# Down products by column quarters for all groups, and row tiles for the last expert's rows

## The chip, the cores and the metric

The kernel runs on one core of one Trainium2 chip. The metric is the device time of one execution in microseconds. Three runs are shown, and one further execution was profiled.

## What is computed

A trunk of two decoder layers over 256 tokens of width 1024, all in float32: retention and a dense SwiGLU, then a short convolution and a mixture of experts, then a final norm. The change lies in the mixture of experts (and in the last additions and the norm behind it):

```python
def _moe_swiglu(xn, w_router, w_gate_e, w_up_e, w_down_e):
    ...
    top_vals, top_idx = lax.top_k(logits, TOP_K)          # 2 of 8 experts for a token
    top_w = jax.nn.softmax(top_vals, axis=-1)
    gates = jnp.sum(jax.nn.one_hot(top_idx, N_EXPERTS, dtype=jnp.float32) * top_w[..., None], axis=1)
    for e in range(N_EXPERTS):
        h = jax.nn.silu(t @ w_gate_e[e]) * (t @ w_up_e[e])        # 1024 -> 3584
        out = out + gates[:, e:e + 1] * (h @ w_down_e[e])         # 3584 -> 1024
```

## The kernel before

Each expert takes up to 96 of its tokens (CAP) into fixed slots, as three groups of 32. A one-hot product (`gather`) brings the tokens into the slots, and at the end another (`scatter`, two products of 512 columns and one addition to `h` on VectorE) brings the slots' rows back to the tokens.

The experts are worked through in 56 steps s, 7 for each expert e (u = 0 to 6), each on 512 of the 3584 hidden columns. In step s TensorE first does gate and up of this step (`moe_gate_up`: 96 products, each with a stationary tile of 128 x 32 and 256 moving columns), then down of the step before (`moe_down`: 48 products). In the profile a product is two instructions. Four products, one for each of TensorE's four column tiles of 32, form a quad. In gate/up the four share their stationary tile, the 32 slots of one group, and take four column ranges of the weights. In down three column tiles belong to the three groups (columns r = 0, 1, 2 of 256), and the fourth takes column quarter 3 for group r:

```python
for r in range(3):
    o = accs[r // 2][:, r % 2 * 256:r % 2 * 256 + 256]
    for t in range(4):
        g, c = (t, r) if t < 3 else (r, 3)
```

So after seven steps the rows of all 96 slots lie in their own partitions for columns 0 to 767, and only quarter 3 lies in partitions 96 to 127, group beside group. `scale_y` (called at the end of step u = 0 of the next expert) copies these to `yraw`, moves them by three transfers of ScalarE's queue (L694) into `yq`, and scales and splits the other 768 columns straight from the accumulators into `yH` and `yL` (the rounded part, on ScalarE, and the remainder, on VectorE). What it returns, `rest`, does the same with `yq`.

Weights come in pieces of 1 MB through 14 buffers (`raw`). Each piece is loaded by SyncE's queue (L107) as soon as TensorE has read the piece that was in its buffer: `moe_piece` stands behind each quarter of gate/up and each half of down. Behind the quarters of gate/up stand the hooks 0 to 3, a table by hand (`extras`): hook 0 transposes the hidden rows of the step before (`moe_hid_T`, with a copy on ScalarE); at u = 1 hooks 1 and 2 scatter the first 512 columns of the expert before, and hook 3 is `rest`; at u = 2 hooks 1 and 2 scatter the other 512. Gathers, slots and gates of the next experts stand in other steps. Instructions run on each engine in the order of the program. The last expert ends with `scale_y`, `scatter`, `rest`, `scatter`, the squares for the norm, and the stores.

Of the kernel before, what the change touches and what calls it, by code (L numbers as in the profile page):

```python
# [53 lines left out]
class Trunk:  # L54
# [20 lines left out]
    def moe_pools(self):  # L75

        self.dense.close()
        pool = lambda name, **k: self.ctx.enter_context(self.tc.tile_pool(name=name, reuse_waits="tile", **k))
        self.xp = pool("x", bufs=1, side="right")
        self.gup = pool("gu", bufs=4, space=bass.MemoryType.PSUM)  # L80
        self.accp = pool("macc", bufs=2, space=bass.MemoryType.PSUM)
        self.psp = pool("mps", bufs=2, space=bass.MemoryType.PSUM)

# [479 lines left out]
    def moe(self, base, ev, mp):  # L563
# [61 lines left out]
        fr = small("fr", [1])  # L625

        def overflow1():
            nc.vector.tensor_scalar(fl, pos, CAP - 0.5, None, op0=OP.is_gt)
            nc.vector.tensor_tensor(fl, fl, sel, op=OP.mult)
            nc.vector.tensor_reduce(fr, fl, axis=AX.XY, op=OP.add)  # L630

        def overflow2():
            p = self.ps()
            self.mm(p[:, 0:1], ones, fr, True, True)
            self.ovf = mp.tile([P, 1], I32, name="ovf")
            return lambda: nc.vector.tensor_copy(self.ovf, p[:, 0:1])
# [47 lines left out]
        def scale_y(e, accs):  # L684


            g = GS[e // 2][0:CAP, e % 2:e % 2 + 1]
            yH, yL = (self.xp.tile([P, D], F32R, name=n) for n in ("yH", "yL"))
            raw = self.xp.tile([P, 768], F32, name="yraw")
            q = self.xp.tile([P, 256], F32, name="yq")  # L690
            nc.vector.tensor_copy(raw[CAP:P, 0:512], accs[0][CAP:P, :])
            nc.vector.tensor_copy(raw[CAP:P, 512:768], accs[1][CAP:P, 0:256])
            for i in range(NG):
                nc.scalar.dma_start(q[32 * i:32 * i + 32], raw[CAP:P, 256 * i:256 * i + 256])  # L694
            for a, n, at in ((accs[0], 512, 0), (accs[1], 256, 512)):
# [41 lines left out]
        def extras(s):  # L737

            e, u = divmod(s, MU)
            pr = e // 2  # L740
            if s == 0:
                return {1: gates1}
            if s == 1:
                return {1: gates2}
            if s == 2:
                return {1: overflow1, 2: lambda: overflow2()()}
            if e and u in (1, 2):
                hf = u - 1
                f = {1: lambda: scatter(e - 1, hf, 0), 2: lambda: scatter(e - 1, hf, 1)}
                if u == 1:  # L750
                    f[3] = late.pop(e - 1)
                elif e % 2 and pr < 3:
                    def nxt():
                        PS[pr + 1] = new_oneh()
                        one_hot(pr + 1, PS[pr + 1])
                        row_factors(pr + 1)
                    f[3] = nxt
                return f
            if u > 2 and (e == 0 or e % 2 and pr < 3):
                a = (0, (1,)) if e == 0 else (pr + 1, (0, 1))  # L760
                f = {q: (lambda kb: lambda: gather(a[0], kb, a[1]))(2 * u - 7 + q) for q in (1, 2)}
                if e == 0 and u == 3:
                    f[3] = lambda: slots(0)
                if e == 0 and u == 4:
                    f[3] = lambda: slot_gates(0)
                return f
            if e and e % 2 == 0 and u == 5:
                return {1: lambda: slots(pr), 2: lambda: slot_gates(pr)}
            return {}

        at = base
        hid = accs = None
        for s in range(MU * NE):
# [5 lines left out]
            if s == COUNT_AT:  # L779
                n_over = nc.values_load(self.ovf[0:1, 0:1], min_val=0, max_val=NE * S)  # L780
            o = self.moe_gate_up(at, XP[e // 2][:, :, e % 2], hooks)
            at += 4
            new = self.moe_swiglu(o)
            if hid is not None:
                if u == 1:
# [42 lines left out]
    def moe_piece(self, at, hook=None):  # L828

        if at not in self.extra:  # L830
            self.dma_next()
        if hook is not None:
            hook()

    def moe_gate_up(self, at, X, hooks):


        A, B = (self.gup.tile([P, 512], F32, name="gu") for _ in range(2))
        o = (A[:, 0:256], A[:, 256:512], B[:, 0:256])
        for q in range(4):  # L840
            w = self.raw[at + q].rearrange("p (k j c) -> p k j c", k=2, j=4)
            for k in range(2):
                kb = 2 * q + k
                for g in range(NG):
# [3 lines left out]
            self.moe_piece(at + q, hooks.get(q))  # L848
        return A.rearrange("p (g u c) -> p g u c", g=2, u=2), B[:, 0:256].rearrange("p (g u c) -> p g u c", g=1, u=2)

    def moe_swiglu(self, o):
        nc = self.nc
        sg, hid = (self.xp.tile([P, NG, P], F32, name=n, bufs=2) for n in ("sg", "hid"))
# [46 lines left out]
    def over(self, low, wm, mp, pos, gts, rs, tH, tL, iota):  # L900
        nc, tc = self.nc, self.tc
        with tc.For_i(0, NE, 1) as e:
# [33 lines left out]
            acc = [self.bank(), self.bank()]  # L936
# [6 lines left out]
            for u in range(MU):  # L943
                o = [self.gup.tile([P, 512], F32, name="gu") for _ in range(2)]
# [165 lines left out]
```

## Time and profile before

| | |
|---|---|
| median of three runs (lowest to highest) | 1546.11 us (1545.5 to 1546.37) |
| profiled execution, its own time | 1545.94 us |
| its span, first to last instruction | 1544.2 us |
| busy: TensorE, weight loads, VectorE, ScalarE | 98%, 67%, 28%, 22% |
| HBM read | 449.68 MB |
| mean granted clock of TensorE | 0.992 |

Times are microseconds from the start of the span. An engine's busy time is the union of its instructions. A granted clock of 1.0 is 2.4 GHz. PE is TensorE, PEld its weight loads, DVE VectorE, ACT ScalarE, POOL GpSimd, SP SyncE; a q behind a name (ACTq, SPq) is the engine's instruction queue, which issues the transfers.

### The profile page before, as it was taken

The page shows a single profiled execution, that of the slowest core. Times are in us where ns is not written, and L with a number is a line of the kernel's source. Part 1 is how long each engine was busy: PE and PEld are TensorE (multiplying, and loading weights), DVE is VectorE, ACT ScalarE, POOL GpSimd, SP SyncE. Part 2 cuts the span into 40 slices and gives each one's busy share as a digit, 9 for nine tenths or more (in the row PEclk, how much of TensorE's full clock was granted, in tenths as well). Part 3 has the DMA queues.
Part 4 walks back from the last instruction along what each step waited for, and adds up shares of the span by engine and source line. Part 5 has one row for each costly group of instructions (what it writes and reads, how often), then busy time and mean ns, then how long its engine had stood idle before and what let it go on. Part 6 is the DMA issues. An engine that isn't in the chain of part 4 may idle for free.

```text
span 1544.2 us, 41832 instructions
## 1 busy us (share of the span) xinstructions
PE 1520.5 (98%) x19502; PEld 1032.4 (67%) x19503; DVE 427.2 (28%) x702; ACT 336.6 (22%) x568; POOL 20.3 (1%) x28
## 2 busy tenths in 40 slices
PE   9999999999999999999999999999999999999995
PEld 7888888888889965555555555555555555555552
DVE  6656665545567630001001001001001101001002
ACT  5444454434454320000000001001001001000001
POOL 0000000000000020000000000000000000000000
PEclk9999999999999999999999999999999999999997
DMA  9845455454545458999999999999999999999960
GB/s 378 357 172 192 140 188 190 179 204 164 191 165 191 178 209 325 341 375 350 354 355 380 384 369 379 346 363 374 365 368 397 352 356 366 371 371 385 358 255 32
DMA packets 65844, 454.28 MB, mean 294 GB/s; under 512 B 7936, under 2 KB 9472, under 8 KB 11520
## 3 DMA queue, kind: packets, MB, share of 16 engines
q1 hardware_dynamic: 63072, 449.34, 76.8%
q8 instruction: 154, 2.52, 0.6%
q10 hardware_dynamic: 2592, 2.20, 0.5%
q14 instruction: 26, 0.21, 0.0%
HBM read 449.68 MB, written 1.05 MB: 292 GB/s over the span
## 4 chain that ended last, share of the span: by engine, by line
PE 97%; DVE 1%; issue 0%; ACT 0%; DMA 0%; POOL 0%; ACTq 0%; SPq 0%; POOLq 0%
PE gu L141 39%; PE acc L141 28%; PE ps L141 27%; PE ps L863 2%; PE ps L331 0%; DMA raw<-in_w 0%; PE ps L188 0%; PE ps L362 0%; PE ps L227 0%; ACT wh L119 0%; POOL xT L809 0%; PE ps L668 0%; ACT junk L208 0%; ACTq L694 0%; PE ps L552 0%
## 5 line engine op out<-in xcount | busy, mean ns | idle before, releaser
L141 PE MATMUL gu<-raw,X 128*32 128x256 f32 x10752 | 615.6, 380 | 0.0
L141 PEld LDWEIGHTS gu<-raw,X 128*32 128x32 f32 x10752 | 336.8, 110 | 232.6 <-issue 20.0
L141 PE MATMUL acc<-raw,hT 128*32 128x256 f32 x5280 | 295.1, 379 | 0.6 <-ACT hT L865 0.6
L141 PEld LDWEIGHTS acc<-raw,hT 128*32 128x32 f32 x5280 | 171.0, 110 | 114.0 <-ACT hT L865 0.9
L122 DVE TENSOR_TENSOR wl<-raw,wh 128x1024 fp32r<-128x1024 f32 x180 | 213.0, 1221 | 39.6 <-ACT wh L119 39.4
L119 ACT ACTIVATE wh<-raw 128x1024 fp32r<-128x1024 f32 x180 | 182.3, 1055 | 80.8 <-PE ps L141 41.7
L141 PE MATMUL ps<-wh,xT 128*128 128x512 f32 x704 | 196.0, 400 | 2.3 <-ACT wh L119 2.3
L141 PEld LDWEIGHTS ps<-wh,xT 128*128 128x128 f32 x704 | 130.7, 189 | 32.5 <-ACT wh L119 2.6
L856 DVE TENSOR_TENSOR hid<-gu,sg 128x256 f32<-128x256 f32 x112 | 34.8, 353 | 397.0 <-ACT sg L855 397.0
L855 ACT ACTIVATE sg<-gu 128x256 f32<-128x256 f32 x112 | 36.7, 330 | 402.9 <-PE gu L141 400.9
L865 ACT ACTIVATE hT<-ps 128x384 f32<-128x384 f32 x56 | 27.4, 490 | 387.6 <-PE ps L863 387.6
L141 PE MATMUL ps<-wl,xT 128*128 128x512 f32 x352 | 111.2, 397 | 0.0
L141 PE MATMUL ps<-xT,wh 128*128 128x256 f32 x640 | 88.8, 280 | 0.5 <-DVE xT L159 0.5
L141 PEld LDWEIGHTS ps<-xT,wh 128*128 128x128 f32 x640 | 81.4, 188 | 1.6 <-ACT xT L157 0.7
L141 PEld LDWEIGHTS ps<-wl,xT 128*128 128x128 f32 x352 | 66.2, 188 | 16.4 <-DVE wl L122 0.5
L651 DVE SCALAR_TENSOR_TENSOR X<-ps,gT,rrow 128x192 f32<-128x192 f32 (+1 forms) x40 | 15.1, 378 | 223.0 <-PE ps L141 222.5
L709 DVE TENSOR_TENSOR h<-h,ps 128x512 f32<-128x512 f32 x32 | 21.9, 688 | 132.2 <-PE ps L141 132.2
L141 PE MATMUL ps<-xT,wl 128*128 128x256 f32 x320 | 50.6, 280 | 0.1
L141 PE MATMUL acc<-wh,hH 128*128 128x512 f32 x112 | 44.0, 393 | 0.0
L141 PE MATMUL acc<-wh,hL 128*128 128x512 f32 x112 | 43.8, 391 | 0.0
L141 PEld LDWEIGHTS ps<-xT,wl 128*128 128x128 f32 x320 | 43.2, 188 | 0.3 <-DVE wl L122 0.3
L141 PE MATMUL acc<-wh,xT 128*128 128x512 f32 x144 | 38.9, 398 | 0.0
(155 smaller groups left out, 754.6 us busy)
## 6 DMA issues: line engine op xcount, KB each, us to landing
raw<-in_w SPq DMA_DIRECT2D x421, 1024.0 KB, 6.5
raw<-in_w SPq DMA_DIRECT2D x6, 512.0 KB, 6.5
xT<-in_w SPq DMA_DIRECT2D x2, 1024.0 KB, 6.0
h<-in_x SPq DMA_DIRECT2D x4, 256.0 KB, 5.0
out<-xT SPq DMA_DIRECT2D x4, 256.0 KB, 2.7
mask<-in_cst ACTq DMA_DIRECT2D x4, 192.0 KB, 4.4
yq<-yraw ACTq DMA_DIRECT2D x24, 32.0 KB, 6.7
xT<-in_gfin SPq DMA_DIRECT2D x1, 512.0 KB, 9.3
```

What stands on the lines that cost most here:

```text
L119: self.nc.scalar.activation(h, r, AF.Copy)
L122: eng.tensor_tensor(l, r, h.bitcast(F32), op=OP.subtract)
L141: self.nc.tensor.matmul(out, lhsT, rhs, start=start, stop=stop)
L651: nc.vector.scalar_tensor_tensor(XP[pr][:, kb, a:b], o, self.gT[:, 3, kb:kb + 1], RR[pr][:, a:b], op0=OP.mult, op1=OP.mult)
L709: nc.vector.tensor_tensor(self.h[:, tb, f], self.h[:, tb, f], p, op=OP.add)
L855: nc.scalar.activation(sg[:, f], p[:, :, 0], AF.Silu)
L856: nc.vector.tensor_tensor(hid[:, f], p[:, :, 1], sg[:, f], op=OP.mult)
L863: self.nc.tensor.transpose(p[:, g], hid[:, g], self.ident)
L865: self.nc.scalar.activation(T, p, AF.Copy)
```

## The change

- Down: column tile q takes column quarter q, for every group. The four products of a quad share their stationary tile.
- So the rows of an expert lie by column quarter in the partitions, and every one has to be moved. `scale_y` copies both accumulators whole, and ScalarE issues twelve transfers (four quarters by three groups, 32 KB each). `rest` scales and splits all 1024 columns. It is hook 2 of u = 1; the scatters are hook 3 of u = 1 and hooks 1 to 3 of u = 2.
- The last expert has no transfers: `last_slots` repeats its slots in four row tiles, and `last_scatter` brings each column quarter to the tokens from the partitions that it lies in.
- In a step the order is now gate/up of groups 0 and 1 (with the hooks), down of groups 0 and 1, down of group 2, gate/up of group 2. The calls of `moe_piece` all stand behind these.
- The gathers and the one-hot of the next pair move to hooks of u = 3 to 5. PSUM tiles become fixed ones, three products with zeros clear banks at the start, and the overflow count becomes nine flags.

```diff
-        self.gup = pool("gu", bufs=4, space=bass.MemoryType.PSUM)
-        self.accp = pool("macc", bufs=2, space=bass.MemoryType.PSUM)
+        gup = pool("gu", bufs=1, space=bass.MemoryType.PSUM)
+        self.gu = [[gup.tile([P, 512], F32, name=f"gu{i}{j}") for j in "ab"] for i in range(2)]
+        self.macc = [gup.tile([P, 512], F32, name=f"macc{i}") for i in range(2)]
         self.psp = pool("mps", bufs=2, space=bass.MemoryType.PSUM)
+        for t in (self.gu[0][1], self.gu[1][1], self.macc[1]):
+            self.nc.tensor.matmul(t, self.zero[:, 0:P], self.zero, start=True, stop=True)
...
-        def scale_y(e, accs):
-
-
-            g = GS[e // 2][0:CAP, e % 2:e % 2 + 1]
-            yH, yL = (self.xp.tile([P, D], F32R, name=n) for n in ("yH", "yL"))
-            raw = self.xp.tile([P, 768], F32, name="yraw")
-            q = self.xp.tile([P, 256], F32, name="yq")
-            nc.vector.tensor_copy(raw[CAP:P, 0:512], accs[0][CAP:P, :])
-            nc.vector.tensor_copy(raw[CAP:P, 512:768], accs[1][CAP:P, 0:256])
-            for i in range(NG):
-                nc.scalar.dma_start(q[32 * i:32 * i + 32], raw[CAP:P, 256 * i:256 * i + 256])
-            for a, n, at in ((accs[0], 512, 0), (accs[1], 256, 512)):
-                f = slice(at, at + n)
-                self.split(yH[0:CAP, f], yL[0:CAP, f], a[0:CAP, 0:n], g)
-            Y[e] = yH, yL
+        def scale_y(e):
+
+            raw = self.xp.tile([P, NG, 256], F32, name="yraw")
+            y = self.xp.tile([P, D], F32, name="y")
+            nc.vector.tensor_copy(raw[:, 0:2].rearrange("p g c -> p (g c)"), self.macc[0])
+            nc.vector.tensor_copy(raw[:, 2], self.macc[1][:, 0:256])
+            for q in range(4):
+                for g in range(NG):
+                    nc.scalar.dma_start(y[32 * g:32 * g + 32, 256 * q:256 * q + 256], raw[32 * q:32 * q + 32, g])
 
             def rest():
-                self.split(yH[0:CAP, 768:D], yL[0:CAP, 768:D], q[0:CAP], g)
+                Y[e] = [self.xp.tile([P, D], F32R, name=n) for n in ("yH", "yL")]
+                self.split(Y[e][0][0:CAP], Y[e][1][0:CAP], y[0:CAP], GS[e // 2][0:CAP, e % 2:e % 2 + 1])
             return rest
+
+        def last_slots(tb):
+
+            if tb == 0:
+                t = self.com.tile([P, 4, NG, P], F32R, name="xT", bufs=3)
+                PT[8], four = t[:, 0:2], t[:, 2:4]
+                PS[8] = four.bitcast(F32)
+                for i in range(2):
+                    o = PS[3].bitcast(F32)[:, i, 1, 0:CAP].rearrange("p (g t) -> p g t", g=NG)
+                    nc.vector.tensor_copy(four[:, i].rearrange("p g (q t) -> p g q t", q=4),
+                                          o[:, :, None, :].to_broadcast([P, NG, 4, 32]))
+            p = self.ps()
+            for g in range(NG):
+                nc.tensor.transpose(p[:, g * P:(g + 1) * P], PS[8][:, tb, g], self.ident)
+            nc.scalar.activation(PT[8][:, tb], p[:, 0:NG * P].rearrange("p (g t) -> p g t", g=NG), AF.Copy)
+
+        def last_gates():
+            p = self.ps()
+            for g in range(NG):
+                for tb in range(2):
+                    self.mm(p[:, g:g + 1], PS[8][:, tb, g], gts[:, tb, 7:8], tb == 0, tb == 1)
+            GS[8] = mp.tile([P, NG], F32, name="gs4")
+            nc.vector.tensor_copy(GS[8], p[:, 0:NG])
+
+        def last_scatter():
+
+
+            yH, yL = (self.xp.tile([P, NG, 256], F32R, name=n) for n in ("yH", "yL"))
+            outs = [self.gu[0] + self.gu[1], self.macc + [self.ps(), self.ps()]]
+            for g in range(NG):
+                src = self.macc[g // 2][:, g % 2 * 256:g % 2 * 256 + 256]
+                self.split(yH[:, g], yL[:, g], src, GS[8][:, g:g + 1])
+            for tb in range(2):
+                for g in range(NG):
+                    for i, y in enumerate((yH, yL)):
+                        for q in range(4):
+                            f = slice(32 * q, 32 * q + 32)
+                            self.mm(outs[tb][q][:, 0:256], PT[8][f, tb, g], y[f, g],
+                                    g == 0 and i == 0, g == NG - 1 and i == 1)
+            return outs
...
-            if u > 2 and (e == 0 or e % 2 and pr < 3):
+                f = {1: gates1}
+            elif s == 1:
+                f = {1: gates2, 2: overflow1}
+            elif s == 2:
+                f = {1: overflow2}
+            elif u == 1:
+                f = {2: late.pop(e - 1), 3: lambda: scatter(e - 1, 0, 0)}
+            elif u == 2:
+                f = {1: lambda: scatter(e - 1, 0, 1), 2: lambda: scatter(e - 1, 1, 0), 3: lambda: scatter(e - 1, 1, 1)}
+            elif u in (3, 4, 5) and (e == 0 or e % 2 and pr < 3):
                 a = (0, (1,)) if e == 0 else (pr + 1, (0, 1))
-                f = {q: (lambda kb: lambda: gather(a[0], kb, a[1]))(2 * u - 7 + q) for q in (1, 2)}
...
+
+                def nxt():
+                    PS[pr + 1] = new_oneh()
+                    one_hot(pr + 1, PS[pr + 1])
+                    row_factors(pr + 1)
+                if e and u == 3:
+                    f[1] = nxt
+                for i in range(2 if u == 3 else 3):
+                    kb = {3: 0, 4: 2, 5: 5}[u] + i
+                    f[i + 2 if u == 3 else i + 1] = (lambda kb: lambda: gather(a[0], kb, a[1]))(kb)
+            elif u == 6 and e % 2 == 0:
+                f = {1: lambda: slots(pr), 2: lambda: slot_gates(pr)}
+            elif e == NE - 1 and u == 5:
+                f = {1: lambda: last_slots(0), 2: lambda: last_slots(1), 3: last_gates}
+            return f
...
-                n_over = nc.values_load(self.ovf[0:1, 0:1], min_val=0, max_val=NE * S)
-            o = self.moe_gate_up(at, XP[e // 2][:, :, e % 2], hooks)
-            at += 4
-            new = self.moe_swiglu(o)
+                n_over = nc.values_load(self.ovf[0:1, 8:9], min_val=0, max_val=1)
+            X = XP[e // 2][:, :, e % 2]
+            self.moe_gate_up(at, X, s, (0, 1), hooks)
+            late_gu = lambda: self.moe_gate_up(at, X, s, (2,), {})
             if hid is not None:
-                if u == 1:
-                    accs = [self.bank(), self.bank()]
-                self.moe_down(at, box["T"], accs, (s - 1) % MU)
-                at += 2
-                if u == 0:
-                    late[e - 1] = scale_y(e - 1, accs)
-            hid = new
+                d = at + 4
+                self.moe_down(d, box["T"], (s - 1) % MU, (0, 1))
+                late_down = lambda: self.moe_down(d, box["T"], (s - 1) % MU, (2,))
+                late_down()
+            late_gu()
+            for i in range(4 if hid is None else 6):
+                self.moe_piece(at + i)
+            at += 4 if hid is None else 6
+            hid = self.moe_swiglu(s)
+            if e and u == 0:
+                late[e - 1] = scale_y(e - 1)
...
-        self.moe_down(at, self.moe_hid_T(hid), accs, MU - 1)
-        last = NE - 1
-        rest = scale_y(last, accs)
+        T = self.moe_hid_T(hid)
+        self.moe_down(at, T, MU - 1, (0, 1, 2))
...
-        for tb in range(2):
-            scatter(last, 0, tb)
-        squares(0)
-        rest()
-        for tb in range(2):
-            nc.gpsimd.tensor_tensor(y[:, tb, cols[0]], self.h[:, tb, cols[0]], gfin[:, cols[0]], op=OP.mult)
-        for tb in range(2):
-            scatter(last, 1, tb)
-        squares(1)
+        outs = last_scatter()
+        for hf in range(2):
+            for tb in range(2):
+                for q in range(2 * hf, 2 * hf + 2):
+                    hs = self.h[:, tb, q * 256:(q + 1) * 256]
+                    nc.vector.tensor_tensor(hs, hs, outs[tb][q][:, 0:256], op=OP.add)
+            squares(hf)
+            if hf == 0:
+                for tb in range(2):
+                    nc.gpsimd.tensor_tensor(y[:, tb, cols[0]], self.h[:, tb, cols[0]], gfin[:, cols[0]], op=OP.mult)
...
-    def moe_gate_up(self, at, X, hooks):
-
-
-        A, B = (self.gup.tile([P, 512], F32, name="gu") for _ in range(2))
...
-                for g in range(NG):
+                for g in groups:
                     for j in range(4):
                         self.mm(o[g][32 * j:32 * j + 32], X[:, kb, 32 * g:32 * g + 32], w[:, k, j],
                                 kb == 0 and g != 1, kb == 7 and g != 0)
-            self.moe_piece(at + q, hooks.get(q))
...
-    def moe_down(self, at, T, accs, u):
+    def moe_down(self, at, T, u, groups):
 
 
         for d in range(2):
-            w = self.raw[at + d].rearrange("p (k c) -> p k c", k=2)
+            w = self.raw[at + d].rearrange("p (k q c) -> p k q c", k=2, q=4)
             for k in range(2):
                 j = 2 * d + k
                 first, last = u == 0 and j == 0, u == MU - 1 and j == 3
-                for r in range(3):
-                    o = accs[r // 2][:, r % 2 * 256:r % 2 * 256 + 256]
-                    for t in range(4):
-                        g, c = (t, r) if t < 3 else (r, 3)
-                        self.mm(o[32 * t:32 * t + 32], T[:, g, 32 * j:32 * j + 32], w[:, k, 256 * c:256 * c + 256],
-                                first and r != 1, last and r != 0)
-            self.moe_piece(at + d)
+                for g in groups:
+                    o = self.macc[g // 2][:, g % 2 * 256:g % 2 * 256 + 256]
+                    for q in range(4):
+                        self.mm(o[32 * q:32 * q + 32], T[:, g, 32 * j:32 * j + 32], w[:, k, q],
+                                first and g != 1, last and g != 0)
```

## Rows read from the trace of the kernel before

**Rows 1.** Page: chain that ended last, share of the span by engine.

```profile
PE 97%; DVE 1%; issue 0%; ACT 0%; DMA 0%; POOL 0%; ACTq 0%; SPq 0%; POOLq 0%
```

**Rows 2.** Waits of the load queue: total us, times, longest.

```profile
SPq L107 <- PE gu L141: 454.6, 162, 18.6
```

**Rows 3.** Chain in order of time, 1500 to 1545: start, us, what.

```profile
1500.57 2.59 PE gu L141 x48
1503.16 0.48 PE ps L863 x3
...
1511.54 5.18 PE acc L141 x96
```

**Rows 4.** Timeline, border of experts 0 and 1: start, us, instructions [idle before <- releaser].

```profile
686.82 5.36 PE L141 MATMUL acc<-raw,hT 128*32 128x256 f32 x96
687.05 0.62 DVE L856 TENSOR_TENSOR hid<-gu,sg 128x256 f32<-128x256 f32 x2 [15.53 <-ACT sg L855]
...
691.82 0.70 DVE L691 COPY yraw<-acc 32x512 f32<-32x512 f32 x1 [4.14 <-PE acc L141]
...
692.55 1.88 ACTq L694 DMA_DIRECT2D yq<-yraw  x3
...
697.91 0.50 PE L141 MATMUL ps<-yH,onehT 96*128 96x512 f32 x1
...
698.58 2.80 PE L141 MATMUL gu<-raw,X 128*32 128x256 f32 x48
...
700.56 0.51 ACT L150 ACTIVATE yH<-yq,gs 96x256 fp32r<-96x256 f32 x1 [4.66 <-DMA yq<-yraw]
```

**Rows 5.** Line 694, the row transfers: issue and landing, min/median/max.

```profile
L694 ACTq DMA_DIRECT2D yq<-yraw x24: 514/553/650, 692.5 to 1524.8; - x24
...
DMA to landing us min/median/max: 1.8/6.7/7.2
```

**Rows 6.** Waits of the load queue, 0 to 60 us.

```profile
SPq L107 <- DMA raw<-in_w: 18.6, 10, 2.5
...
SPq L107 <- DMA cs<-in_cst: 5.7, 1, 5.7
```

**Rows 7.** Transfers, 4 to 40 us: totals; issues with KB and us to landing.

```profile
DMA packets 3089, 14.59 MB, mean 405 GB/s; under 512 B 553, under 2 KB 809, under 8 KB 1724
...
raw<-in_w SPq DMA_DIRECT2D x16, 1024.0 KB, 13.1
...
gR<-in_router ACTq DMA_DIRECT2D x1, 32.0 KB, 10.4
```

**Rows 8.** Page: groups of instructions, busy us and mean ns of one.

```profile
L122 DVE TENSOR_TENSOR wl<-raw,wh 128x1024 fp32r<-128x1024 f32 x180 | 213.0, 1221 | 39.6 <-ACT wh L119 39.4
L119 ACT ACTIVATE wh<-raw 128x1024 fp32r<-128x1024 f32 x180 | 182.3, 1055 | 80.8 <-PE ps L141 41.7
```

**Rows 9.** Stretches: us, busy by engine, granted clock, DMA share, GB/s.

```profile
8.00:20.00 12.00, 11.21 (x44) 8.56 (x45) 7.51 (x17) 7.70 (x17) 0.00 (x0) 0.86 1.03 423
546.00:550.00 4.00, 2.67 (x24) 2.58 (x24) 3.35 (x8) 2.89 (x7) 3.05 (x3) 0.85 0.60 250
550.00:554.00 4.00, 3.77 (x12) 2.31 (x14) 1.75 (x11) 0.00 (x0) 0.60 (x1) 0.50 0.00 0
554.00:558.00 4.00, 3.82 (x21) 2.66 (x19) 1.84 (x6) 0.00 (x0) 0.00 (x0) 0.80 0.00 0
1523.00:1526.00 3.00, 0.23 (x6) 0.00 (x0) 0.91 (x2) 0.56 (x1) 0.00 (x0) 1.00 0.09 22
1528.00:1530.00 2.00, 0.00 (x0) 0.00 (x0) 0.78 (x2) 1.76 (x5) 1.74 (x2) 0.61 0.00 0
```

**Rows 10.** Timeline of the tail, as rows 4.

```profile
1529.60 0.49 ACT L150 ACTIVATE yH<-yq,gs 96x256 fp32r<-96x256 f32 x1
...
1534.31 0.16 DVE L814 TENSOR_TENSOR rfin<-ss 128x2 f32<-128x2 f32 x1 [0.85 <-ACT junk L803]
```

**Rows 11.** Groups by form, 566 to 1545.

```profile
L141 PE MATMUL ps<-gts,oneh 128*128 128x1 f32 x32 | 4.2, 253 | 0.0
```

More of the change, by code (lines that the diff above doesn't have):

```diff
@@ L624, in moe @@
         fl = small("fl", [2, 8])
-        fr = small("fr", [1])
+        fr = small("fr", [9])
         def overflow1():
+            nc.vector.tensor_scalar(fl, pos, 63.5, None, op0=OP.is_gt)
+            nc.vector.tensor_tensor(fl, fl, sel, op=OP.mult)
+            nc.vector.tensor_tensor(fr[:, 0:8], fl[:, 0], fl[:, 1], op=OP.add)
             nc.vector.tensor_scalar(fl, pos, CAP - 0.5, None, op0=OP.is_gt)
             nc.vector.tensor_tensor(fl, fl, sel, op=OP.mult)
-            nc.vector.tensor_reduce(fr, fl, axis=AX.XY, op=OP.add)
+            nc.vector.tensor_reduce(fr[:, 8:9], fl, axis=AX.XY, op=OP.add)
         def overflow2():
             p = self.ps()
-            self.mm(p[:, 0:1], ones, fr, True, True)
-            self.ovf = mp.tile([P, 1], I32, name="ovf")
-            return lambda: nc.vector.tensor_copy(self.ovf, p[:, 0:1])
+            self.mm(p[:, 0:9], ones, fr, True, True)
+            self.ovf = mp.tile([P, 9], I32, name="ovf")
+            nc.vector.tensor_scalar(self.ovf, p[:, 0:9], 0.5, None, op0=OP.is_gt)
         PT, XP, GS, RR = {}, {}, {}, {}
@@ L740, in extras @@
             pr = e // 2
+            f = {}
             if s == 0:
[L742 to L749, printed above, removed]
-                if u == 1:
[L751 to L758, printed above, removed]
@@ L759, in extras @@
-            if u > 2 and (e == 0 or e % 2 and pr < 3):
-                a = (0, (1,)) if e == 0 else (pr + 1, (0, 1))
-                f = {q: (lambda kb: lambda: gather(a[0], kb, a[1]))(2 * u - 7 + q) for q in (1, 2)}
[L762 to L768, printed above, removed]
@@ L769, in extras @@
-            return {}
+                f = {1: gates1}
[8 more added lines that the diff above has]
+            elif u in (3, 4, 5) and (e == 0 or e % 2 and pr < 3):
+                a = (0, (1,)) if e == 0 else (pr + 1, (0, 1))
+                def nxt():
[11 more added lines that the diff above has]
+                f = {1: lambda: last_slots(0), 2: lambda: last_slots(1), 3: last_gates}
@@ L771, in moe @@
+            return f
         at = base
-        hid = accs = None
+        hid = None
         for s in range(MU * NE):
@@ L826, in moe, with moe_piece, moe_gate_up @@
         self.fallback(n_over, mp, pos, gts, rs, tH, tL, iota)
-    def moe_piece(self, at, hook=None):
+    def moe_piece(self, at):
         if at not in self.extra:
             self.dma_next()
-        if hook is not None:
-            hook()
-    def moe_gate_up(self, at, X, hooks):
-        A, B = (self.gup.tile([P, 512], F32, name="gu") for _ in range(2))
+    def moe_gate_up(self, at, X, s, groups, hooks):
+        A, B = self.gu[s % 2]
         o = (A[:, 0:256], A[:, 256:512], B[:, 0:256])
@@ L847, in moe_gate_up, with moe_swiglu @@
                                 kb == 0 and g != 1, kb == 7 and g != 0)
-            self.moe_piece(at + q, hooks.get(q))
-        return A.rearrange("p (g u c) -> p g u c", g=2, u=2), B[:, 0:256].rearrange("p (g u c) -> p g u c", g=1, u=2)
-    def moe_swiglu(self, o):
+            if q in hooks:
+                hooks[q]()
+    def moe_swiglu(self, s):
         nc = self.nc
-        sg, hid = (self.xp.tile([P, NG, P], F32, name=n, bufs=2) for n in ("sg", "hid"))
+        A, B = self.gu[s % 2]
+        o = (A.rearrange("p (g u c) -> p g u c", g=2, u=2), B[:, 0:256].rearrange("p (g u c) -> p g u c", g=1, u=2))
+        sg, hid = (self.xp.tile([P, NG, P], F32, name=n, bufs=b) for n, b in (("sg", 1), ("hid", 2)))
         for p, f in zip(o, (slice(0, 2), slice(2, 3))):
@@ L935, in over @@
             nc.vector.tensor_copy(gs, pg[:, 0:2])
-            acc = [self.bank(), self.bank()]
+            acc = self.macc
             wt = self.com.tile([P, 2048], F32, name="xT", bufs=3)
@@ L943, in over @@
             for u in range(MU):
-                o = [self.gup.tile([P, 512], F32, name="gu") for _ in range(2)]
+                o = self.gu[0]
                 for q in range(4):
```

1 line of the change is left out of this document (removed).

## The prediction

> **What bounds the kernel now.** I read the page first: the shares by engine and the chain that ended last. TensorE is busy 98% of the span (the table above), and 97% of the chain is its own work [rows 1]. So an edit changes the time only if it changes TensorE's work, makes TensorE wait, or touches the head or the tail. The 1 MB weight loads looked like a second bound, so the waits of the load queue came next: it waits for TensorE to free a buffer, 454.6 us over 162 times for one tile alone [rows 2]. The loads run ahead, and TensorE sets the pace.
>
> Then the chain near the end, for the price of one product. 48 gate/up instructions take 2.59 us and 96 down instructions take 5.18 us [rows 3]: 54.0 ns each for both. Today a down quad has four different stationary tiles, and a gate/up quad has one stationary tile four times against four column ranges. The changed down products have the second pattern. Since both patterns cost 54.0 ns and the count stays at 48 products (96 instructions) in a step, I cost the new mapping, and the split of the groups into (0, 1) and (2), at nothing. A step is 288 instructions x 54 ns plus 0.5 us of transposes, 16.1 us.
>
> Last I read a border between two experts as a timeline. It shows what TensorE consumes from the drained accumulators, and when [rows 4].
>
> **The change at an expert's border.** Let T0 be the end of the first step (u = 0) of expert e. That is when the changed kernel calls scale_y(e-1).
>
> TensorE's side. After T0 come the four quarters of groups (0, 1), each 32 instructions (1.73 us), with the transposes behind the first (0.48 us [rows 3]). So the scatter of hook 3 is reached at T0 + 7.4. Undisturbed it takes 0.67 us (697.91 to 698.58 [rows 4]), until T0 + 8.07. Before, the first scatter needed no transferred row, and the transferred quarter was wanted only a step later.
>
> The data's side. Everything now goes through the transfers:
> - Group 2 of gate/up now ends the step, so the second half of the SwiGLU starts at T0. Both halves ended 0.85 us after their products (686.82 to 687.67), and the first copy of the accumulator takes 0.70 us [rows 4]. The first transfer can be issued at T0 + 1.55.
> - A transfer costs ScalarE 514 to 650 ns to issue [rows 5]. Three took 1.88 us [rows 4], so I take 0.61 us each. There are now 12 where there were 3. The last begins at 1.55 + 11 x 0.61 = T0 + 8.3. The copy of the transposed hidden rows stands behind them on ScalarE, but it is wanted only after the scatter.
> - A transfer landed 6.7 us after its issue (median), 1.8 us with no load beside it [rows 5]. At the border it was 6.4 to 8.0 us from the first issue to its reader (692.55 to 700.56 [rows 4]). With 6.4 the last lands at T0 + 14.7.
> - Then rest() splits all 1024 columns at once, ScalarE 1.06 us and, after it, VectorE 1.22 us (the prices of 1024-column splits, [rows 8]). With hand-overs and the last scatter product, TensorE goes on at T0 + 17.5.
>
> That is a stall of 17.5 - 8.07 = 9.4 us: the lower bound.
>
> The upper bound comes from the waits at the kernel's start. A weight load there waits for the landing of earlier loads, 10 times, and once 5.7 us for cs, a transfer of ScalarE's queue that it has no data from [rows 6]. So an issue can have to wait until some earlier, unrelated transfer is down. With about 405 GB/s and 13.1 us to landing [rows 7] there were 13.1 x 405 = 5.3 MB in flight, some five loads, so the number outstanding is limited to not many more. At the new border, six loads (freed between T0 - 2.6 and T0, since all six calls of moe_piece now stand at the end of the step) and twelve small transfers come together. If a late small one must wait for the last of the six (issued within 1 us of T0, landing 13.1 us later, about T0 + 14.0 [rows 7]) and five issues follow from there, the last begins at T0 + 16.5 and lands 1.8 us later, because no load is left beside it. TensorE goes on 2.8 us after that, at T0 + 21.1: a stall of 13.0 us. How many transfers back the wait reaches no row says, so I take the middle, 11.2 us.
>
> The stall has a tail. The granted clock was still 1.00 in the first 3 us of the pause at the end, and its mean was 0.61 in 1528 to 1530, behind some 5 us of little work [rows 9]. A fall lasts: a mean of 0.86 over the 12 us from 8 on is 12 x 0.14 / 0.5 = 3.4 us at 0.50, and the means of 546 to 558 make (0.15 + 0.50 + 0.20) x 4 / 0.5 = 6.8 us at 0.50, most of it under busy work [rows 9]. A pause of 9 us should thus be followed by 3.4 to 6.8 us at 1.2 instead of 2.4 GHz, losing half of that: 1.7 to 3.4 us, I take 2.5.
>
> Seven experts go this way (the eighth does not): 7 x (11.2 + 2.5) = 96 us; bounds 7 x (9.4 + 1.7) = 78 and 7 x (13.0 + 3.4) = 115.
>
> On issuing, the Trainium skill ("DMA: Bandwidth & Descriptors", section "Issuing engines are not separate DMA queues") says that the sequencer's time to start a transfer is usually small beside the transfer. This trace differs: 0.55 us a time, times twelve, is as long as a landing. By the rule, the change would cost far less; that is the first rival.
>
> **The other parts.** The last expert's row tiles: six transposes (two hooks, 1.0 us) and six gate products of N = 1; 32 instructions of such products took 4.2 us [rows 11], so 12 take 1.6 us and, with what their weight loads add, some 2.3. Together +3.3 us. The three products that clear banks: +0.7 us at most. In the last step the SwiGLU's end is no longer under the down products: +0.85 us. In return the tail no longer waits for a transfer. Today the transferred quarter is first read at 1529.60 and the squares are done at 1534.31 [rows 10]; with three splits, 48 short products and eight additions instead I estimate 1 to 4 us less, and take 2.7. Sum: +2, between 0 and +4. The counters of overflow (three more small VectorE operations), the moved gathers and the moved one-hot cost nothing: VectorE stood idle for 15.5 us before the SwiGLU's product of the border [rows 4], and such idle time covers them; uncovered, each would cost under 1 us. The copies by which PT[8] is built also start before TensorE asks.
>
> The burst of six loads: a step needs 6.29 MB in 16.2 us, 388 GB/s, and the queue moved 405 where it was full [rows 7]. Eight buffers stay ahead, and each stall lets the loads catch up: nothing.
>
> **Sum.** The profiled execution took 1545.94 us (1.7 us of it around the span of 1544.2), beside a median of 1546.11. 1545.9 + 96 + 2 = 1644 us; with the bounds, 1545.9 + 78 + 0 = 1624 to 1545.9 + 115 + 4 = 1665.
>
> **Rivals.**
> - *Issuing is cheap.* If the 12 issues ran as one, all would land by T0 + 8.2, TensorE would go on at T0 + 11.0, and 2.9 us x 7, without a fall of the clock, gives 1546 + 21 + 2 = 1569. Against it: 514 ns is the smallest issue seen [rows 5].
> - *The transfers are hidden, and the tail decides: not slower, or faster.* This needs the last row to land by T0 + 4.9, 2.5 us ahead of hook 3. From that point the border costs nothing, and the tail's saving of up to 4 us less 3.3 + 0.7 remains: 1545 to 1548. For it: before, the scatter of the border never waited. Against it: at 0.61 us an issue, no more than six of the twelve have begun by T0 + 4.9.
> - *Small transfers alternate with whole loads.* One load takes about 2.6 us at 405 GB/s; 12 x 2.6 = 31 us puts the last landing at T0 + 33 and the stall at 28 us: 1546 + 7 x 30.5 + 2 = 1761. For it: a 32 KB transfer took 10.4 us at the start with the queue full [rows 7]. Against it: the third of a border would then land 5.2 us later after its issue than the first, but 24 transfers landed 6.7 us after theirs in the median and 7.2 at most [rows 5].
> - *The loads become the bound.* Buffers come free only in the last sixth of a step. If the queue ran dry by 0.9 us a step, 49 steps would add 44 us: 1688. Against it: eight pieces ahead, and a pause at every border.
>
> **How the numbers follow.** Forecast 0.76, cheap issue 0.05, hidden 0.03, alternating 0.05, loads the bound 0.08, others 0.03. The likeliest case's own range is 1624 to 1665. I widen it to 1612 and 1688, for the loads' case above and shorter waits below; about 2 in 10 remain outside. Under 0.2% (3 us) a measurement cannot tell this kernel from no change. Only the hidden case lies within that or below: faster 0.01, same 0.02, slower 0.97.
>
> **What would show it.** In the changed profile, TensorE idles 8 to 13 us once in each of seven borders, in front of the first scatter product, released by ScalarE's yH and then VectorE's yL; ScalarE issues 84 transfers; if the wait for loads is real, the last issues of a border stand apart from the first. The granted clock falls behind each stall. Down instructions stay at 54 ns. The prediction is wrong if the scatter is not held, if the twelve issues take under 5 us and land at once, or if TensorE waits for raw.

## The result, and the profile after

The changed kernel takes 1639.57 us (median of four runs, 1638.83 to 1646.88) beside 1545.99 us for the kernel before: a ratio of 1.0616, 95% interval 1.0586 to 1.0646. The forecast was 1644 us, in a range of 1612 to 1688.

The page of the profile after: TensorE's busy time and share of the span, and the issues of transfers with KB and us to landing.

```profile
PE 1541.3 (94%) x19564; PEld 1037.1 (63%) x19564; DVE 427.8 (26%) x696; ACT 335.3 (20%) x556; POOL 20.3 (1%) x28
...
raw<-in_w SPq DMA_DIRECT2D x421, 1024.0 KB, 9.1
...
y<-yraw ACTq DMA_DIRECT2D x84, 32.0 KB, 5.2
```

TensorE is busy 94% of a span of 1637.9 us, not 98% of 1544.2. What it waits for stands in its list of waits (us in total, times, longest):

```profile
PE ps L144 <- ACT yH L153: 72.8, 7, 11.1
PE ps L144 <- DVE yL L154: 3.6, 7, 0.5
```

Seven waits for yH and seven for the yL behind it make 76.4 us, 10.9 at each border, and no wait for weights (raw) stands in the list. The first of these borders as a timeline, answering to [rows 4]:

```profile
689.07 3.64 PE L144 MATMUL gu1b<-raw,X 128*32 128x256 f32 x64
...
692.52 1.91 PE L144 MATMUL gu0a<-raw,X 128*32 128x256 f32 x32
...
693.29 0.68 DVE L695 COPY yraw<-macc 128x512 f32<-128x512 f32 x1
...
694.01 9.13 ACTq L699 DMA_DIRECT2D y<-yraw  x12
...
694.37 0.55 PE L908 MATMUL ps<-ident,hid 128*128 128x128 f32 x3
...
694.84 5.39 PE L144 MATMUL gu0a<-raw,X 128*32 128x256 f32 x96
703.46 0.49 ACT L910 ACTIVATE hT<-ps 128x384 f32<-128x384 f32 x1 [10.41 <-issue]
709.52 1.15 ACT L153 ACTIVATE yH<-y,gs 96x1024 fp32r<-96x1024 f32 x1 [5.57 <-DMA y<-yraw]
...
710.70 1.28 DVE L154 SCALAR_TENSOR_TENSOR yL<-y,gs,yH 96x1024 fp32r<-96x1024 f32 x1 [16.40 <-ACT yH L153]
...
710.72 0.79 PE L144 MATMUL ps<-yH,onehT 96*128 96x512 f32 x1 [10.49 <-ACT yH L153]
...
712.04 0.80 PE L144 MATMUL ps<-yL,onehT 96*128 96x512 f32 x1 [0.52 <-DVE yL L154]
...
712.76 7.05 PE L144 MATMUL macc<-raw,hT 128*32 128x256 f32 x96
```

T0 is 692.52. TensorE has done its four quarters at 700.23 (694.84 + 5.39). ScalarE's queue issues from 694.01 to 703.14, and only then does ScalarE make the copy hT. yH begins when the last transfer is down, at 709.52, and yL has to wait for yH. Down goes on at 712.76, T0 + 20.2.

The granted clock around the wait (stretch, busy by engine, granted clock, DMA share, GB/s), answering to [rows 9]:

```profile
692.00:700.00 8.00, 8.00 (x147) 4.51 (x137) 1.22 (x3) 0.28 (x1) 0.00 (x0) 1.00 0.82 321
700.00:710.00 10.00, 0.23 (x7) 0.00 (x0) 0.00 (x0) 0.97 (x2) 0.00 (x0) 0.63 0.90 318
710.00:720.00 10.00, 8.76 (x106) 4.32 (x110) 2.31 (x3) 0.94 (x2) 0.00 (x0) 0.69 0.05 19
720.00:730.00 10.00, 10.00 (x166) 5.21 (x155) 0.98 (x2) 0.77 (x2) 0.00 (x0) 1.00 0.99 392
```

In 710 to 720 TensorE is busy again, and its mean clock is 0.69: 10 x 0.31 / 0.5 = 6.2 us at 1.2 instead of 2.4 GHz. The 96 down instructions behind the wait took 7.05 us, not 5.36.

### The profile page after: what moved, and what is told of

It reads as the page before. It is cut to its first block, busy times and chain, and to the rows that moved or that the text cites. A ratio compares the mean times of both kernels' runs of the same rounds, so it can differ in the third digit from the quotient of the medians.

```text
span 1637.9 us, 41959 instructions
## 1 busy us (share of the span) xinstructions
PE 1541.3 (94%) x19564; PEld 1037.1 (63%) x19564; DVE 427.8 (26%) x696; ACT 335.3 (20%) x556; POOL 20.3 (1%) x28
## 5 line engine op out<-in xcount | busy, mean ns | idle before, releaser
L144 PE MATMUL macc<-raw,hT 128*32 128x256 f32 x5280 | 307.9, 391 | 0.6 <-ACT hT L910 0.6
L144 PEld LDWEIGHTS macc<-raw,hT 128*32 128x32 f32 x5280 | 171.7, 113 | 125.2 <-issue 18.1
L144 PE MATMUL gu0a<-raw,X 128*32 128x256 f32 x3584 | 210.5, 381 | 0.0
L144 PE MATMUL gu1a<-raw,X 128*32 128x256 f32 x3584 | 207.8, 380 | 0.0
L144 PEld LDWEIGHTS gu1a<-raw,X 128*32 128x32 f32 x3584 | 111.5, 110 | 77.9 <-issue 7.6
L144 PEld LDWEIGHTS gu0a<-raw,X 128*32 128x32 f32 x3584 | 110.2, 110 | 76.5 <-issue 8.4
L144 PE MATMUL gu1b<-raw,X 128*32 128x256 f32 x1792 | 101.8, 379 | 0.0
L144 PE MATMUL gu0b<-raw,X 128*32 128x256 f32 x1792 | 101.8, 379 | 0.0
L144 PEld LDWEIGHTS gu1b<-raw,X 128*32 128x32 f32 x1792 | 57.8, 110 | 38.9
L144 PEld LDWEIGHTS gu0b<-raw,X 128*32 128x32 f32 x1792 | 57.6, 110 | 39.1
```

The source lines that it names most:

```text
L144: self.nc.tensor.matmul(out, lhsT, rhs, start=start, stop=stop)
```

## The experiments

The waits below are TensorE's for yH and yL over the seven borders, read from each kernel's list of waits. e2, e4, e5, e6, e8, e10 and e12 are single executions. A ratio is taken against executions of the kernel before made beside the run; they spread from 1544 to 1551 us, so a ratio need not be that of two times in this table.

| kernel | time, us | waits for yH and yL, us |
|---|---|---|
| before | 1545.99 | none at the seven borders |
| changed | 1639.57 | 76.4 |
| e3, no transfers | 1544.96 | none |
| e2, issued, landing not waited for | 1604.37 | 39.3 |
| e12, loads held back | 1606.72 | 40.7 |
| e5, six transfers | 1596.08 | 34.2 |
| e6, old order | 1614.29 | 49.0 |
| e4, two queues | 1655.89 | 88.0 |
| e10, loads behind in program order | 1644.08 | 78.6 |
| e1, late scatters | 1585.47 | none, but 24.3 for hT |
| e8, e1 and hT by VectorE | 1548.16 | none |
| e9, e1 and issues behind hT | 1547.78 | none |
| e11, e9 and one-hots first | 1542.84 | none |
| e7, before with the last expert's part | 1544.88 | none |

### Is it the border alone? (e3_no_transfers, e2_no_landing)

```diff
+            nc.gpsimd.memset(raw[:, 3], 0.0)
-            for q in range(4):
-                for g in range(NG):
-                    nc.scalar.dma_start(y[32 * g: ...], raw[32 * q: ..., g])     # e3 only
...
-                self.split(..., y[0:CAP], ...)
+                self.split(..., raw[0:CAP].rearrange("p g c -> p (g c)"), ...)   # e3 and e2
```

Both let `rest` split the copied rows where they lie. e2 still issues the twelve transfers, e3 issues none; "the kernel before this one" in the next paragraph is e2.

> Edit: as the kernel before this one, and the twelve transfers are not issued at all (the output is not the reference's). Theory: rest is ready at about T0 + 5.5, before hook 3 at T0 + 7.4; no wait; 1541 to 1549 us, the rest of the change costing about nothing. Rival (split and copies at the border alone are too late, or the new step order costs): 1555 us or more.

Measured: 1544.96 us, ratio to before 0.9981 (0.9968 to 0.9995), no wait at the borders. So all the rest of the change together (column mapping, step order, late loads, row tiles, moved hooks) costs nothing; by the interval it saves 1 to 5 us. The profiled spans add up: 1543.3 here and 1637.9 changed differ by 94.6, of which 76.4 are waits and 17.8 are TensorE's longer busy time (1523.5 to 1541.3), at a mean granted clock of 0.967 instead of 0.993.

> Edit: the twelve transfers are issued as before, but rest splits the copied accumulators in place (rows of the wrong slots and a quarter of zeros, so the output is not the reference's); only the landing is no longer waited for. Theory (issue and landing add up): the split starts when ScalarE has issued all twelve and copied the transposed rows, about T0 + 10.6, TensorE goes on at about T0 + 13.4, a wait of some 5 us at each border, and 1585 to 1600 us. Rival (landing alone decides, the issues are hidden): no wait, under 1553 us. Rival (issues alone decide): as the changed kernel, over 1625 us.

Measured: 1604.37 us in one run, 4 above the range. Issues and landing both count: without the landing about half of the waiting stays,

```profile
PE ps L144 <- ACT yH L153: 35.3, 7, 6.0
PE ps L144 <- DVE yL L154: 4.0, 7, 0.8
```

5.6 us a border. Both rivals fall.

### What makes the chain so long? (e5_six, e12_loads_held, e10_loads_behind, e4_two_queues)

e5 leaves out half of the transfers:

```diff
-            for q in range(4):
+            for q in range(2):
...
-                self.split(Y[e][0][0:CAP], Y[e][1][0:CAP], y[0:CAP], ...)
+                self.split(h, l, y[0:CAP, None, 0:512].to_broadcast([CAP, 2, 512]), ...)
```

> Edit: six of the twelve transfers (quarters 0 and 1); rest reads those 512 columns twice, so its size stays (the output is not the reference's). Theory (issue, with its waits, and landing add up): the last issue begins about 4 to 5 us earlier, the landing behind it stays 5 to 7 us, each wait is near 6 us instead of 11: 1590 to 1605 us. Rival (landing behind the six loads decides): 1625 us or more. Rival (issue alone): about 1575 us or less.

Measured: 1596.08 us, waits 34.2 us. Six transfers fewer shorten each wait by (76.4 - 34.2) / 7 = 6.0 us, 1.0 us each. That is more than the 0.6 us of an issue. Most of the rest are the issues' own waits: the six take 4.1 us a border (mean of seven) where the twelve take 9.7, 0.9 us for each one fewer.

e12 takes the loads away from the transfers, without touching the transfers: the six buffers of the border step get a later reader.

```diff
+                        rest()
+                        for i in range(6):
+                            nc.scalar.activation(self.junk[:, i:i + 1], self.raw[a + i][:, 0:1], AF.Copy)
+                            self.moe_piece(a + i)
```

> Edit: the changed kernel, but the six loads of a border step are held back until rest has split the rows: ScalarE reads one element a row of each of the six buffers behind its split, so the buffers come free only then. Eight pieces lie ahead, so TensorE should not run out of weights. Theory (the loads in flight make the issues wait and the landing long): the twelve issues run without a wait (the last begins 6.7 us after the first) and the last lands about 2 us after its issue instead of 5 to 7; the split starts some 9 us after the first issue instead of 15, TensorE waits about 5 us a border instead of 11: 1585 to 1602 us. Rival (issue and landing are as long without loads): 1630 to 1645 us.

Measured: 1606.72 us, 5 above the range. The direction and most of the size hold: landing took 1.9 us in the median instead of 5.2, as the issues of this kernel show,

```profile
y<-yraw ACTq DMA_DIRECT2D x84, 32.0 KB, 1.9
```

and the twelve issues take less time. Rows from the timelines of the first border and of the fifth, where SyncE's queue issues too:

```profile
696.25 7.99 ACTq L699 DMA_DIRECT2D y<-yraw  x12
...
705.74 1.15 ACT L153 ACTIVATE yH<-y,gs 96x1024 fp32r<-96x1024 f32 x1 [0.69 <-DMA y<-yraw]
...
1210.72 7.62 ACTq L699 DMA_DIRECT2D y<-yraw  x12
...
1214.47 12.20 SPq L110 DMA_DIRECT2D raw<-in_w  x7
...
1222.31 1.15 ACT L153 ACTIVATE yH<-y,gs 96x1024 fp32r<-96x1024 f32 x1 [3.44 <-DMA y<-yraw]
```

At the first border the last issue ends at 704.24, and yH begins 1.5 us later. At the fifth it ends at 1218.34, and yH begins 4.0 us later. There a load of the step before is issued at 1214.47, in the middle of the twelve. SyncE's waits in 1214 to 1215 show what had held it, and its issue shows how long it was under way:

```profile
SPq L110 <- DMA y<-yraw: 19.7, 1, 19.7
...
raw<-in_w SPq DMA_DIRECT2D x1, 1024.0 KB, 5.3
```

The load had waited 19.7 us for a small transfer, and it landed at about 1219.8; the small transfers behind it landed later still. Such a load falls between the small transfers at three of the seven borders, and the waits there are 6.3 to 7.1 us. At the other four they are 4.6 to 5.7 us, as the theory has it. These three borders make the waits 5 us longer than seven of the other kind would be; this edit does not hold such loads back. The waits fall by 76.4 - 40.7 = 36 us, the time by 33: about that much of the loss is due to the six loads in flight.

e10 tried the same by program order alone:

```diff
+            if not (e and u == 0):
+                for i in range(n):
+                    self.moe_piece(at + i)
...
                 late[e - 1] = scale_y(e - 1)
+                for i in range(n):
+                    self.moe_piece(at + i)
```

> Edit: the changed kernel, with the border step's six loads behind the twelve transfers in program order. Theory (an issue waits for the landing of the transfer eight places before it, and the landing of small transfers is long because of the loads in flight): if the loads now take their place behind, they wait for small transfers, the twelve issues run with no wait and land in 2 to 3 us, TensorE waits about 5 us a border: 1580 to 1600 us. Rival (the place in program order does not reach the queues, or loads in flight play no part): 1630 to 1645 us.

Measured: 1644.08 us, as the changed kernel. The buffers come free as early as in the changed kernel, and in the trace three of the six loads are still issued ahead of the first transfer (687.97 to 689.70, and 693.53); the order of the lines in the program does not hold them. This run says nothing on the loads' part; e12 does.

e4 gives half of the issues to SyncE's queue.

```diff
-                    nc.scalar.dma_start(
+                    (nc.scalar if g % 2 == q % 2 else nc.sync).dma_start(
```

> Edit: six of the twelve transfers of a border are issued by SyncE's queue, six by ScalarE's, in turn; same bytes. Theory (the time to issue is a large part): the last issue begins 3 to 4 us earlier, and each wait is shorter by as much: 1600 to 1618 us. Rival (the landing behind six loads decides, whenever the transfer is issued): 1632 to 1645 us. Rival (the transfers on SyncE's queue stand behind loads that wait): longer, over 1645 us.

Measured: 1655.89 us, slower: the third case. The issues of the first border, start and length in us, ScalarE's and SyncE's:

```profile
695.38 4.11 ACTq L699 DMA_DIRECT2D y<-yraw  x6
...
698.68 3.66 SPq L110 DMA_DIRECT2D raw<-in_w  x3
...
702.43 3.80 SPq L699 DMA_DIRECT2D y<-yraw  x6
711.20 1.15 ACT L153 ACTIVATE yH<-y,gs 96x1024 fp32r<-96x1024 f32 x1 [11.18 <-DMA y<-yraw]
```

ScalarE is through at 699.49, but SyncE's six stand behind three loads that wait themselves, begin at 702.43 and end at 706.23, 10.85 us behind the first one; the twelve on one queue took 9.13. ScalarE's own time to issue was halved, and the last issue came later than with one queue.

### What does the order of a step do? (e6_old_order)

```diff
-            self.moe_gate_up(at, X, s, (0, 1), hooks)
...
+            self.moe_gate_up(at, X, s, (0, 1, 2), hooks)     # a load behind each quarter
+            at += 4
+            new = self.moe_swiglu(s)
+            if hid is not None:
+                self.moe_down(at, box["T"], (s - 1) % MU, (0, 1, 2))
+                at += 2
```

> Edit: the order of a step and the places of the loads go back to those of before (gate/up of all groups with a load behind each quarter, then down of all groups); column mapping, twelve transfers, hooks and tail stay. Theory (order and loads only set how much cover the chain has): hook 3 is reached 3.5 us later and the first issue comes about 0.8 us earlier against it, so each wait shrinks by 4 to 6 us: 1590 to 1612 us. Rival (the new order and its burst of loads are the cause): under 1565 us. Rival (they play no part): over 1630 us.

Measured: 1614.29 us, 2 above the range; the waits shrink by (76.4 - 49.0) / 7 = 3.9 us a border. The new order costs cover; that it costs no time of its own is e3's result.

### Can the chain be covered? (e1_late_scatter, e8_T_on_vector, e9_issue_later, e11_one_hot_first)

```diff
             elif u == 1:
-                f = {2: late.pop(e - 1), 3: lambda: scatter(e - 1, 0, 0)}
+                f = {}                                    # e9: {1: issue}
             elif u == 2:
-                f = {1: lambda: scatter(e - 1, 0, 1), 2: ..., 3: ...}
+                f = {1: late.pop(e - 1), 3: lambda: scatter(e - 1, 0, 0)}
...
+            if e and u == 3:      # the other three scatters, before (e11: behind) what the hook holds
```

> Edit: rest moves from hook 2 of u = 1 to hook 1 of u = 2, and the four scatters to hook 3 of u = 2 and hooks 1 to 3 of u = 3; mapping, twelve transfers, step order and loads stay. Theory (the whole loss is TensorE waiting at the border for rows that land about 17 us behind T0, and the low clock behind that wait): the rows are asked for at T0 + 20 and later, no wait, 1543 to 1550 us. Rival (the column mapping, the step order or the late loads cost time in every step): most of the loss stays, over 1590 us.

Measured: 1585.47 us, ratio to before 1.0245 (1.0217 to 1.0273): neither theory. The scatters wait no more, but another wait is there:

```profile
PE macc L144 <- ACT hT L919: 24.3, 8, 4.2
PE ps L144 <- DVE oneh L605: 4.4, 3, 1.5
```

Its timeline at the first border:

```profile
695.25 9.51 ACTq L699 DMA_DIRECT2D y<-yraw  x12
...
696.09 5.39 PE L144 MATMUL gu0a<-raw,X 128*32 128x256 f32 x96
...
705.09 0.49 ACT L919 ACTIVATE hT<-ps 128x384 f32<-128x384 f32 x1 [10.79 <-issue]
...
705.63 0.20 PEld L144 LDWEIGHTS macc<-raw,hT 128*32 128x32 f32 x8 [4.64 <-ACT hT L919]
```

hT, the copy that down multiplies with, stands on ScalarE behind the twelve issues (695.25 to 704.76), and TensorE, done with its quarters at 701.5, waits 4.16 us for it. In the changed kernel the longer wait for yH covers this one. e8 and e9 test that reading. e8 is e1 with the copy hT made by VectorE at u = 1; e9 is in the cut above.

> Edit: e1_late_scatter, and at u = 1 the copy of the transposed hidden rows is made by VectorE instead of ScalarE. Theory (what e1 has left is the down products' wait for that copy, which stands behind the twelve issues on ScalarE): both waits gone, 1543 to 1549 us. Rival (late loads or the transfers' traffic slow TensorE as well): 1560 us or more.

> Edit: e1_late_scatter, and the twelve issues move from the border to hook 1 of u = 1, behind the copy of the transposed hidden rows on ScalarE's queue. Theory: neither the scatter (asked for at T0 + 24) nor down (its copy is ahead of the issues) waits; 1542 to 1548 us, as without transfers. Rival (twelve issues block something else on ScalarE, or loads that wait for small transfers starve TensorE): 1560 us or more.

Measured: 1548.16 us and 1547.78 us (ratio 0.9999, 0.9988 to 1.0009). Both remove the wait, by different means, so it was the order on ScalarE's queue. e9 still issues all twelve, beside the same loads, in 11.36 us at the first border; ScalarE is blocked for that time, and TensorE waits for nothing of it. It keeps the second row of e1 (DVE oneh, 4.4 us): the one-hot of the next pair stood behind the scatter's addition on VectorE. e11 turns these two around.

> Edit: e9_issue_later, and where a hook holds a one-hot or a gather and a scatter, the scatter comes second. Theory (what e9 has left is three waits of row_factors for the one-hot, 4.4 us, which stands behind a scatter's addition on VectorE): they go, and the span comes within 1 us of the kernel without transfers: 1541 to 1545 us, below the kernel before. Rival (the transfers' traffic costs the rest): as e9.

Measured: 1542.84 us (1541.23 to 1543.19), ratio to before 0.9973 (0.9962 to 0.9984). Its border:

```profile
696.50 0.49 ACT L922 ACTIVATE hT<-ps 128x384 f32<-128x384 f32 x1 [1.90 <-PE ps L920]
696.56 11.14 ACTq L701 DMA_DIRECT2D y<-yraw  x12
...
701.59 5.36 PE L144 MATMUL macc<-raw,hT 128*32 128x256 f32 x96
...
713.85 1.15 ACT L153 ACTIVATE yH<-y,gs 96x1024 fp32r<-96x1024 f32 x1 [0.71 <-DMA y<-yraw]
...
717.86 0.19 PEld L144 LDWEIGHTS ps<-yH,onehT 96*128 96x128 f32 x1 [0.41 <-issue]
```

The copy is ahead of the issues, and the waits for the one-hot are gone from the list. yH is ready at 715.0, and the scatter asks for it at 717.86. This version beats the kernel before by 3.4 us (its slowest run of seven lies under the fastest of 19 of the kernel before) and the changed one by 97.

### Is the row tile of the last expert a gain by itself? (e7_hybrid)

```diff
-                        g, c = (t, r) if t < 3 else (r, 3)
+                        g, c = (r, t) if quarters else (t, r) if t < 3 else (r, 3)   # quarters: last expert only
```

with last_slots, last_gates, last_scatter and the additions behind it put into the kernel before.

> Edit: the kernel before, with the new parts for the last expert alone (its down products by column quarters, last_slots, last_gates, last_scatter and the additions behind it); the other seven keep their three transfers and the old order. Theory (the last expert's part is a small gain: the tail 4 to 5 us shorter, its extra slots and gates 3 us longer): 1 to 3 us under the kernel before. Rival (the extra products and transposes eat it): no difference, within 0.05%, or slower.

Measured: 1544.88 us beside 1546.23 (ratio 0.999, 0.998 to 1.000): 1.35 us less, at the edge of the noise.

## Why the prediction was right

**TensorE sets the pace, and the mapping costs nothing: right.** e3 shows it, and 96 down instructions behind no wait still take 5.36 us (at e11's border), as in [rows 4].

**A wait in front of the first scatter: right, place and size.** I forecast 11.2 us a border between 9.4 and 13.0; the lists show 10.9. By steps: first issue at T0 + 1.55 forecast, 694.01 - 692.52 = 1.49 measured; hook 3 reached at 7.4 forecast, 7.7 measured; TensorE on its way again at 17.5 to 21.1 forecast, 20.2 measured. The split was somewhat longer, 1.15 + 1.28 us, not 1.06 + 1.22.

**The time to issue and land: right in the sum, wrong in the story of the upper bound.** I had the last small transfers wait for the last of the six loads and then land in 1.8 us with nothing beside them. In the trace the twelve issues take 9.13 us, so they wait only some 2 us, and the landing behind them takes 6.4 us (703.14 to 709.52). Below are the issues from the eighth on with the loads beside them (start and length in us); then the us to landing, of the first transfer (694.01) and of the loads and transfers issued about 700.3 to 703:

```profile
700.05 3.08 ACTq L699 DMA_DIRECT2D y<-yraw  x5
700.42 1.53 SPq L110 DMA_DIRECT2D raw<-in_w  x3
...
y<-yraw ACTq DMA_DIRECT2D x1, 32.0 KB, 6.0
...
raw<-in_w SPq DMA_DIRECT2D x3, 1024.0 KB, 8.1
y<-yraw ACTq DMA_DIRECT2D x5, 32.0 KB, 5.7
```

The eighth issue begins at 700.05, when the first transfer is down (694.01 + 6.0): the unrelated earlier transfer that it had to wait for was a small one, not the last load. Three of the six loads were issued from 688.45 on, T0 - 4.1 and not the T0 - 2.6 that I had. The other three follow at 700.42 and are in flight while the last small ones land. At e12's first border, without loads of that step, yH begins 1.5 us behind the last issue. It is rather the loads that wait for the small transfers, as SyncE's waits show:

```profile
SPq L110 <- PE macc L144: 691.4, 100, 17.0
...
SPq L110 <- DMA y<-yraw: 66.8, 9, 11.3
```

Nine waits, 66.8 us; the kernel before has none for its yq. The middle between my two bounds was near the truth with neither bound's mechanism: less waiting at issue than in the upper, a loaded landing as in the lower. That the middle came out within 0.3 us of the measured wait was luck.

**The Trainium skill's rule on issuing** ("DMA: Bandwidth & Descriptors", section "Issuing engines are not separate DMA queues"), that the sequencer's time is usually small beside the transfer: for one transfer this trace agrees, 601 ns in the median of 84 issues beside 5.2 us to landing. For twelve in a row it does not help: e2, which waits for the issues but not for the landing behind them, keeps 59 of the 95 us by which the changed kernel lies above e3. A second issuing engine did not help either: e4 is slower.

**The low clock: right.** 2.5 us a border forecast, 17.8 / 7 = 2.5 measured as TensorE's longer busy time against e3.

**The rivals: none holds.** The issues were not cheap (9.13 us for twelve), the waits were not hidden (76.4 us), and TensorE's list of waits never names raw, so the loads are not the bound. Small transfers did not alternate with whole loads: the 84 landed within 7.5 us of their issue at most,

```profile
DMA to landing us min/median/max: 1.8/5.2/7.5
```

**The other parts: mis-sized.** I took +2 us; e3 shows 1 to 5 us less than before. The tail is the term: the norm's sum (rfin) began 11.4 us after what first reads the last down product before (1522.87 to 1534.31, [rows 10]), and 6.7 us after it in the changed kernel. The first row is of the kernel before, the others of the changed one:

```profile
1522.87 0.70 DVE L691 COPY yraw<-acc 32x512 f32<-32x512 f32 x1 [10.65 <-PE acc L141]
...
1616.77 5.39 PE L144 MATMUL macc<-raw,hT 128*32 128x256 f32 x96 [0.58 <-ACT hT L910]
1621.79 0.47 ACT L153 ACTIVATE yH<-macc,gs 128x256 fp32r<-128x256 f32 x1 [5.08 <-PE macc L144]
...
1628.49 0.16 DVE L859 TENSOR_TENSOR rfin<-ss 128x2 f32<-128x2 f32 x1 [1.03 <-ACT junk L847]
```

From 1621.79 to 1628.49 are 6.7 us, so 4.7 us are saved where I took 2.7. And I charged 3.3 us for the last expert's slots and gates, which I didn't measure by themselves; e7, with both terms and neither order nor transfers, comes out 1.35 us under the kernel before.

**What I named but did not price:** the copy of the transposed rows behind the twelve issues. In the changed kernel it is covered, as forecast; e1 and e9 show that it is worth 38 us (1585.47 - 1547.78) when the cover goes.

## What to carry to other kernels

Before rows are sent through small transfers, count the issues as work of the engine that issues them, and look at what stands behind them on its queue: here twelve issues of 0.6 us blocked a copy that TensorE needed, and only the larger wait in front hid that. A chain of copies, issues, landing and splits need not be short if the reader can be moved: the same twelve transfers cost 95 us when their rows were asked for 7.7 us behind the border, and nothing when they were issued behind that copy and asked for 24 us behind the border. When a wait has been removed, read the list of waits again, for the one it covered.

## What the runs showed of the hardware

- A pause of TensorE cost about as much clock at half its length. Against e3 (1523.5 us busy, mean granted clock 0.993) TensorE's busy time rose by 17.8 us with seven waits of 10.9 us (0.967), and by 20.2 us in e2 with seven of 5.6 us (0.978). Still shorter pauses cost somewhat less: e1, with seven of 3.4 us (24.3 us less the 0.6 at the end that every kernel here has; 0.985), was 12.5 us longer busy than e9 (1521.0), which has no such waits.
- Small transfers on one queue and loads on another hold each other up. Transfers of 32 KB landed in 5.2 us (median of 84) beside the loads, and in 1.9 us in e12, without those of the border step. Loads wait for small transfers with which they share no data: 66.8 us in nine waits in the changed kernel, and one load of e12 19.7 us.
